# A two-layer hybrid decoder step on one core: the border chain in steps, the end of mixing reordered, the sampled convolution traced first

## The chip, the cores and the metric

The kernel runs on one core of a Trainium2 chip. The metric is the time of one execution in microseconds on the device; lower is better. The engines are PE (TensorE, matmuls), DVE (VectorE), ACT (ScalarE), POOL (GpSimd) and SP (SyncE, which here only issues DMAs).

## The reference

One inference step of a trunk of two layers. 512 prompt rows and 32 sampled rows (8 sequences of 4 tokens) go through the same weights. Each layer mixes tokens in four groups of width 256 (a convolution of width 31, a gated MLP, differential attention, pooling), projects the four back and adds; then follows a SwiGLU network of hidden width 2816.

```python
def hybrid_layer(x, pos, conv_prev, pool_prev, attend, lam_init, p):
    h = rms_norm(x, p['g_mix_pre'])
    z = h @ p['w_in']                                        # 1024 -> 2048
    a, ga, u, vb, q, k, v, xd = jnp.split(z, IN_SPLITS, axis=-1)
    ya, conv_new = conformer_conv(a, ga, conv_prev, ...)     # width 31, LayerNorm, silu
    yb, v_rows = chunk_sgu(gelu(u), gelu(vb), ...)
    o = attend(q, k, v, lam)
    yc = rms_norm(o, p['attn_sub_g'], LN_EPS) * (1.0 - lam_init)
    yd, pool_new = pool_mix(xd, pool_prev, pos, p['pool_w'], p['pool_scale'])
    mix = jnp.concatenate([ya, yb, yc, yd], axis=-1) @ p['w_out']
    x = x + rms_norm(mix, p['g_mix_post'])
    gate, up = jnp.split(rms_norm(x, p['g_ffn_pre']) @ p['w_gu'], 2, axis=-1)
    x = x + rms_norm((silu(gate) * up) @ p['w_down'], p['g_ffn_post'])
    return x, k, v, conv_new, pool_new, v_rows
```

The sampled rows use paged keys and values, and the last 30 convolution inputs and 15 pooling inputs of their sequences (`state_conv`, `state_pool`); the new states are outputs.

## The kernel before

Every product of float32 numbers is made of three: activations and weights are each split into a rounded part and the rest (`xhi`, `xlo`; `whi` by ACT, L194, and `wlo` by DVE or POOL, L197). `xhi` and `xlo` hold the activations of all 544 rows with the model dimension on the partitions: columns 0 to 511 are the prompt's four tiles of 128 rows, 512 to 543 the sampled rows. `turn` (L236 to 242) fills them for one tile: PE transposes, an ACT cast to `xhi`, a DVE subtraction to `xlo`.

The code is traced with Python generators that hand each other the turn. A planner in the compiler then draws up the order of each engine's queue: it takes what its own model says is ready, and among that what was traced first (`high_priority` moves work up). Every engine then works through its queue in order, and instructions wait on semaphores. So the place of a piece in the trace is a preference, not a position.

A layer has two stages. In `mixing` the prompt's 512 rows go through `w_in`, in halves: for each block of 128 output columns first the rows 0 to 255, then rows 256 to 543, with the sampled ones (`B0, BN = 256, 288`). Beside it run `conv`, `attention`, `gating` and `pooling`, one step at a time (`advance`); `conv` becomes urgent once its 60 taps (L427) are traced. Their outputs are `Y[0]` to `Y[3]` (ya, yb, yc, yd), split by `hilo` (ACT L351, DVE L352). At its end `conv` normalises four tiles (`xn`, L455), turns them back (L461), scales them and applies tanh (ACT L463, L464), and forms ya by a DVE product (L465). `pooling` adds windows for the two halves of its channels (L645), subtracts the mean (L662 to 665) and multiplies by a small matrix on PE. `gating` ends with a Gelu on ACT (L619) and the product u times gate (DVE L623).

The second stage is `prompt` with `sample` beside it. `project_last` makes `w_out` (eight turns of 24 matmuls; `W_OUT_TURNS` goes through tiles and halves, and within one, `W_OUT_ORDER`: yc, ya, yd, yb), with square (ACT L1299) and product by the gain (DVE L1300). After a tile's second half `finish` does the first norm (`ss`, `rsqrt`, x_t at L1318), squares (ACT L1323), does the second norm (L1326) and turns the tile. `rsqrt` is a DVE step (L177) and a power on POOL (L178). The weights of the second half go into a ring (`ring2`) in a pool that opens after mixing's. The gate and up blocks and `w_down` follow. After each piece the main loop moves `sample` on: `sample_conv`, `sample_gate` and `sample_pool` in rounds, then attention over the cache with gathers by POOL, then the sampled feed-forward part.

`sample_conv` loads two state pieces of 120 rows (tag `pr`, two buffers, shared with the other two), turns them (L875), forms the new inputs (L880), stores the new state rows (L886 to 890: a POOL copy, a PE turn, an ACT copy, a DMA), then does 60 taps on DVE (L894, L897) and a LayerNorm.

At the layer border the last `w_down` product ends with `finish` for each tile, and for the sampled rows with `finish_sample` (L244 to 265): a product with a selector adds four partial sums, then square and gain (L253, L254), first norm (L257), square (L261), second norm (L263) and the turn. It is traced after tile 3's `finish`; its inputs are there before. Then mixing of the next layer starts with four first halves; PSUM has two banks `acc` and two banks `s` for them.

## Time and profile before

| what | us |
|---|---|
| three timed runs | 1435.68, 1439.87, 1442.28 |
| their median | 1439.87 |
| the profiled execution | 1446.75 |
| its span, first to last instruction | 1445.1 |
| PE busy in it | 1389.1 |
| DVE busy | 818.4 |

The profile is one execution; its rows carry a start in microseconds from the span's start. Layer 0's mixing ends near 180 and its out-projection near 240; the border to layer 1 lies near 740; layer 1's mixing ends near 900.

### The profile page before, as it was taken

Reading aid. Unit: us, or ns where it says so; the run is one execution under the profiler, and the core shown is the slowest. Engines: PE = TensorE matmul, PEld = TensorE weight load, DVE = VectorE, ACT = ScalarE, POOL = GpSimd, SP = SyncE. Lnnn points to the kernel's source line nnn. Section 1 sums busy time; section 2 is a strip of 40 time slices with the busy share of each in tenths; the row PEclk is TensorE's granted clock in tenths of the full one; section 3 lists DMA queues with packets and bytes.
Section 4 is the critical chain, followed back from the end, with each engine's and each line's share of the span. In section 5 each row is a group of like instructions: output and inputs, shape, how many; then the busy total and the mean of one; then the engine's idle time right before and its main releaser. Section 6 shows DMA issues by size and latency. Waiting matters only on the chain.

```text
span 1445.1 us, 22960 instructions
## 1 busy us (share of the span) xinstructions
PE 1389.1 (96%) x9274; PEld 1089.5 (75%) x9274; DVE 818.4 (57%) x1652; ACT 488.9 (34%) x962; POOL 213.5 (15%) x245
## 2 busy tenths in 40 slices
PE   6999798999999999999979997999999999999997
PEld 6987687876666777777879876888766667778775
DVE  5996677876433233333759856778664332333345
ACT  4346543332233222222433454334222332222231
POOL 1001124454200000000000011244442000000000
PEclk9999899999999999999989978999999999999999
DMA  7320334889768721314522203367876796213132
GB/s 215 96 89 30 127 130 158 295 319 330 246 215 272 225 91 59 117 59 150 188 69 75 74 30 125 128 218 264 330 293 241 222 296 213 71 61 114 59 135 91
DMA packets 155171, 235.60 MB, mean 163 GB/s; under 512 B 8880, under 2 KB 116346, under 8 KB 155066
## 3 DMA queue, kind: packets, MB, share of 16 engines
q1 hardware_dynamic: 130378, 157.34, 33.5%
q0 software_dynamic: 18496, 67.18, 12.7%
q10 hardware_dynamic: 6192, 9.61, 1.8%
q8 instruction: 73, 1.20, 0.3%
q14 instruction: 32, 0.26, 0.1%
HBM read 222.07 MB, written 12.04 MB: 162 GB/s over the span
## 4 chain that ended last, share of the span: by engine, by line
PE 81%; DVE 8%; DMA 4%; issue 3%; ACT 2%; POOL 2%; SPq 0%; POOLq 0%; DVEq 0%; ACTq 0%
PE acc L128 63%; PE sx L128 9%; PE ps L128 3%; PE s L128 3%; DMA kr<-in_cache_k_dram,ik 2%; DVE sca L897 2%; PE oT L128 1%; DMA vr<-in_cache_v_dram,iv 1%; DVE wlo L197 1%; PE ps L521 1%; POOL kr L1011 1%; DVE xlo L242 1%; PE ps L239 1%; DVE m L1326 1%; DVE x_t L1318 1%
## 5 line engine op out<-in xcount | busy, mean ns | idle before, releaser
L128 PE MATMUL acc<-xhi,whi 128*128 128x512 f32 (+2 forms) x1152 | 408.8, 356 | 1.1 <-ACT zs L403 0.8
L128 PE MATMUL acc<-xlo,whi 128*128 128x512 f32 (+2 forms) x1152 | 405.0, 352 | 1.1 <-DVE xlo L242 1.1
L128 PE MATMUL acc<-xhi,wlo 128*128 128x512 f32 (+2 forms) x1152 | 405.8, 353 | 0.0
L194 ACT CAST whi<-raw 128x1024 fp32r<-128x1024 f32 x178 | 184.7, 1048 | 378.3 <-PE acc L128 349.1
L197 DVE TENSOR_TENSOR wlo<-raw,whi 128x1024 fp32r<-128x1024 f32 x172 | 214.8, 1255 | 170.8 <-ACT whi L194 169.1
L128 PEld LDWEIGHTS acc<-xhi,whi 128*128 128x128 f32 x1152 | 219.2, 191 | 44.4 <-issue 11.2
L128 PEld LDWEIGHTS acc<-xhi,wlo 128*128 128x128 f32 x1152 | 219.2, 190 | 33.0 <-issue 6.8
L128 PEld LDWEIGHTS acc<-xlo,whi 128*128 128x128 f32 x1152 | 219.5, 191 | 31.5 <-issue 3.9
L128 PE MATMUL acc<-whi,h 128*128 128x512 f32 x704 | 223.7, 396 | 0.0
L128 PEld LDWEIGHTS acc<-whi,h 128*128 128x128 f32 x704 | 131.1, 188 | 42.9 <-issue 9.5
L178 POOL TENSOR_TENSOR rsw<-rsw,mhalf 128x1 f32<-128x1 f32 (+2 forms) x62 | 36.6, 594 | 795.1 <-DVE rsw L177 769.3
L128 PE MATMUL acc<-wlo,h 128*128 128x512 f32 x352 | 138.2, 394 | 0.0
L1014 DVE STREAM_TRANSPOSE kt<-kr 128x1024 f32<-128x1024 f32 x64 | 78.0, 1232 | 23.6 <-DMA kr<-in_cache_k_dram,ik 19.5
L427 DVE SCALAR_TENSOR_TENSOR cacc<-hext,pf,cacc 128x512 f32<-128x512 f32 x120 | 86.7, 746 | 0.7
L1011 POOL DMA_INDIRECT kr<-in_cache_k_dram,ik x64 | 69.4, 1084 | 88.0 <-DVE kt L1014 71.5
L128 PEld LDWEIGHTS acc<-wlo,h 128*128 128x128 f32 x352 | 66.1, 188 | 17.7 <-issue 4.1
L1370 DVE SCALAR_TENSOR_TENSOR th<-th,acc 128x512 f32<-128x512 f32 (+1 forms) x46 | 29.7, 646 | 85.2 <-PE acc L128 85.1
L1041 POOL DMA_INDIRECT vr<-in_cache_v_dram,iv x64 | 62.5, 977 | 71.5 <-PE sx L128 55.1
L128 PE MATMUL sx<-vr,pt 128*32 128x256 f32 x512 | 46.5, 383 | 1.2 <-DMA vr<-in_cache_v_dram,iv 1.2
L1179 DVE SCALAR_TENSOR_TENSOR sth<-sth,ps 128x64 f32<-128x64 f32 x22 | 4.8, 220 | 71.4 <-ACT sth L1178 71.4
L128 PE MATMUL sx<-kt,qs 128*32 128x128 f32 x1024 | 43.9, 277 | 0.7 <-DVE kt L1014 0.7
L1372 ACT CAST h<-th 128x512 fp32r<-128x512 f32 (+1 forms) x48 | 27.9, 582 | 48.3 <-DVE th L1370 48.2
(426 smaller groups left out, 1790.3 us busy)
## 6 DMA issues: line engine op xcount, KB each, us to landing
raw<-in_w_gu_dram SPq DMA_DIRECT2D x44, 1024.0 KB
raw<-in_w_down_dram SPq DMA_DIRECT2D x20, 1024.0 KB
rws<-in_w_gu_dram SPq DMA_DIRECT2D x40, 512.0 KB
raw<-in_w_in_dram SPq DMA_DIRECT2D x16, 1024.0 KB
raw<-in_w_out_dram SPq DMA_DIRECT2D x8, 1024.0 KB
rwo<-in_w_out_dram SPq DMA_DIRECT2D x16, 512.0 KB
rws<-in_w_down_dram SPq DMA_DIRECT2D x16, 512.0 KB
x<-x_t ACTq DMA_DIRECT2D x12, 512.0 KB
```

What stands on the lines that cost most here:

```text
L128: T.matmul(out, lhsT, rhs, start=start, stop=stop)
L178: G.tensor_tensor(y, v, mhalf[:P, :n], op=ALU.pow)
L194: S.copy(hi, src)
L197: eng.tensor_tensor(lo, src, hi.bitcast(F32), op=ALU.subtract)
L239: T.transpose(ov[:, c, :], src[:P, 128 * (4 * b + c):128 * (4 * b + c) + 128], ident[:P, :P])
L427: V.scalar_tensor_tensor(a, hext[c][:, t:t + SEQ], pf[:, 8 + 2 * t + c:9 + 2 * t + c], a, op0=ALU.mult, op1=ALU.add)
L897: V.scalar_tensor_tensor(a[:, c], ext[:, c, :, t:t + 4], pf[:, 8 + 2 * t + c:9 + 2 * t + c], a[:, c], op0=ALU.mult, op1=ALU.add)
L1011: G.indirect_dma_start(out=kr, out_offset=None, in_=ck, in_offset=bass.IndirectOffsetOnAxis(ap=ik[:, s, bg:bg + 1], axis=0))
L1014: V.transpose(kt, kr)
L1041: G.indirect_dma_start(out=v.rearrange("p t e -> p (t e)"), out_offset=None, in_=cv, in_offset=bass.IndirectOffsetOnAxis(ap=iv[:, s, a:a + ...
L1370: V.scalar_tensor_tensor(th[:, :n], th[:, :n], 0.5, ou[:, :n], op0=ALU.mult, op1=ALU.mult)
L1372: S.copy(hh, th[:, :n])
```

## The change

Four things. `finish_sample` becomes a generator of six steps, and at the border of layer 0 these are traced between the steps of tile 3's `finish` (`beside`). In `pooling` the first two adds of the second half of the channels are queued behind conv's last normalised tile on DVE, and traced after it. In `gating` the last products and their splits are traced after conv's last ya product and queued behind it on DVE. `issue_after` sets an order within one queue only, without a wait for the end. In `sample_conv` both states are loaded in one round, the taps come ahead of the stores of the state rows, and there are three rounds of taps and not seven. The extra buffers of `rsw` for the tag `q` keep the two chains' roots apart.

```diff
--- before.py
+++ after.py
@@ -172,7 +172,7 @@
 
     def rsqrt(pool, src, P, n, scale, eps, tag):
 
-        w = pool.tile([128, 2, n], F32, tag=f"rs{tag}{n}", bufs={"m": 4, "p": 3}.get(tag, 1) if n == 1 else 1, name="rsw")
+        w = pool.tile([128, 2, n], F32, tag=f"rs{tag}{n}", bufs={"m": 4, "p": 3, "q": 2}.get(tag, 1) if n == 1 else 1, name="rsw")
         v, y = w[:P, 0, :], w[:P, 1, :]
         V.tensor_scalar(v, src, scale, eps, op0=ALU.mult, op1=ALU.add)
         G.tensor_tensor(y, v, mhalf[:P, :n], op=ALU.pow)
@@ -244,6 +244,10 @@
     def finish_sample(fp, parts, m_s, x_t, stage, gpo, gpr, dst, tag):
 
 
+        for _ in finish_sample_steps(fp, parts, m_s, x_t, stage, gpo, gpr, dst, tag):
+            pass
+
+    def finish_sample_steps(fp, parts, m_s, x_t, stage, gpo, gpr, dst, tag):
         ss = fp.tile([128, 4], F32, name="sums_s")[:NT]
         junk = fp.tile([128, DM], BF16, name="junk_s")
         for half in range(2):
@@ -252,15 +256,20 @@
             hs = slice(512 * half, 512 * half + 512)
             S.activation(junk[:NT, hs], o[:NT, :], AF.Square, accum_out=ss[:, half:half + 1])
             V.tensor_tensor(m_s[:, hs], o[:NT, :], gpo[:NT, hs], op=ALU.mult)
+        yield
         V.tensor_tensor(ss[:, 2:3], ss[:, 0:1], ss[:, 1:2], op=ALU.add)
         r = rsqrt(fp, ss[:, 2:3], NT, 1, 1.0 / DM, RMS_EPS, tag)
+        yield
         V.scalar_tensor_tensor(x_t, m_s, r, x_t, op0=ALU.mult, op1=ALU.add)
         SY.dma_start(x_at(stage + 1)(SEQ, NT), x_t)
         if gpr is None:
             return
         S.activation(junk[:NT], x_t, AF.Square, accum_out=ss[:, 3:4])
+        yield
         r = rsqrt(fp, ss[:, 3:4], NT, 1, 1.0 / DM, RMS_EPS, tag)
+        yield
         V.scalar_tensor_tensor(m_s, x_t, r, gpr[:NT], op0=ALU.mult, op1=ALU.mult)
+        yield
         if dst is None:
             turn(m_s, NT, SEQ)
             return
@@ -452,7 +461,9 @@
                 for c in range(2):
                     T.transpose(o[:, 128 * c:128 * c + 128], out[c][:, 128 * t:128 * t + 128], ident)
                 mean, r = ln_stats(mp, o[:, :256], 128, "m")
-                V.tensor_scalar(xn[:, t, :], o[:, :256], mean, r, op0=ALU.subtract, op1=ALU.mult)
+                flow["xn"] = V.tensor_scalar(xn[:, t, :], o[:, :256], mean, r, op0=ALU.subtract, op1=ALU.mult).ins
+                if t == 3:
+                    done.add("xn")
                 yield
             y = yp.tile([128, 2, 2, SEQ], F32R, tag="y", name="ya")
             for c in range(2):
@@ -462,8 +473,10 @@
                 zh, th = out[c], hext[c][:, 0:SEQ]
                 S.activation(zh, o, AF.Identity, scale=pf[:, 72 + c:73 + c], bias=pf[:, 74 + c:75 + c])
                 S.activation(th, zh, AF.Tanh)
-                V.scalar_tensor_tensor(zh, th, 1.0, zh, op0=ALU.add, op1=ALU.mult)
+                flow["za"] = V.scalar_tensor_tensor(zh, th, 1.0, zh, op0=ALU.add, op1=ALU.mult).ins
                 hilo(y, c, zh)
+                if c == 1:
+                    done.add("za")
                 yield
             Y[0] = y
 
@@ -618,10 +631,13 @@
                 yield
             S.activation(uv[:, 0:2], uv[:, 0:2], AF.Gelu)
             S.activation(zs[:, 4:6, :], zs[:, 4:6, :], AF.Gelu)
+            while "za" not in done:
+                yield
             for c in range(2):
                 tf = uv[:, 2 + c, :]
-                V.tensor_tensor(tf, tf, uv[:, c, :], op=ALU.mult)
-                hilo(y, c, tf)
+                with tc.issue_after(flow["za"]):
+                    V.tensor_tensor(tf, tf, uv[:, c, :], op=ALU.mult)
+                    hilo(y, c, tf)
                 yield
             Y[1] = y
 
@@ -647,6 +663,11 @@
                 d = dext[c]
                 s2 = mp.tile([128, 528], F32, tag="pl", bufs=3, name="s2")
                 wn = mp.tile([128, 528], F32, tag="pl", bufs=3, name="wn")
+                held = ExitStack()
+                if c == 1:
+                    while "xn" not in done:
+                        yield
+                    held.enter_context(tc.issue_after(flow["xn"]))
                 if c == 0:
                     add(s2[hi, 0:526], d[hi, 0:526], d[hi, 1:527])
                     add(wn[lo, 0:SEQ], d[lo, 14:526], d[lo, 15:527])
@@ -655,6 +676,7 @@
                     add(s2[:, 0:526], d[:, 0:526], d[:, 1:527])
                     s4 = mp.tile([128, 528], F32, tag="pl", bufs=3, name="s4")
                     add(s4[:, 0:524], s2[:, 0:524], s2[:, 2:526])
+                    held.close()
                     add(wn[lo, 0:SEQ], s4[lo, 8:520], s4[lo, 12:524])
                     add(s2[hi, 0:520], s4[hi, 0:520], s4[hi, 4:524])
                     add(wn[hi, 0:SEQ], s2[hi, 0:SEQ], s2[hi, 8:520])
@@ -875,10 +897,18 @@
                 T.transpose(o[:, 120 * c:120 * c + 120], st[:, 128 * c:128 * c + 128], ident[:120, :120])
             for c in range(2):
                 S.copy(ext[:, c, 4 * hf:4 * hf + 4, 0:30], o[:, 120 * c:120 * c + 120].rearrange("p (s t) -> p s t", s=4))
-            yield
         for c in range(2):
             V.scalar_tensor_tensor(ext[:, c, :, 30:34], zs[:, 2 + c, :].rearrange("p (s t) -> p s t", s=NS), 1.0,
                                    zs[:, c, :].rearrange("p (s t) -> p s t", s=NS), op0=ALU.add, op1=ALU.mult)
+        a = mp.tile([128, 2, NS, 4], F32, tag="sca", name="sca")
+        for c in range(2):
+            V.tensor_scalar(a[:, c], ext[:, c, :, 0:4], pf[:, 8 + c:9 + c], pf[:, c:c + 1], op0=ALU.mult, op1=ALU.add)
+        for t in range(1, CW):
+            for c in range(2):
+                V.scalar_tensor_tensor(a[:, c], ext[:, c, :, t:t + 4], pf[:, 8 + 2 * t + c:9 + 2 * t + c], a[:, c],
+                                       op0=ALU.mult, op1=ALU.add)
+            if t % 10 == 0:
+                yield
         for hf in range(2):
             o = ps()
             for c in range(2):
@@ -889,15 +919,6 @@
             S.copy(cn[:120, :256], o[:120, :256])
             S.dma_start(O[8][l, 4 * hf:4 * hf + 4].rearrange("s t c -> (s t) c"), cn[:120, :256])
             yield
-        a = mp.tile([128, 2, NS, 4], F32, tag="sca", name="sca")
-        for c in range(2):
-            V.tensor_scalar(a[:, c], ext[:, c, :, 0:4], pf[:, 8 + c:9 + c], pf[:, c:c + 1], op0=ALU.mult, op1=ALU.add)
-        for t in range(1, CW):
-            for c in range(2):
-                V.scalar_tensor_tensor(a[:, c], ext[:, c, :, t:t + 4], pf[:, 8 + 2 * t + c:9 + 2 * t + c], a[:, c],
-                                       op0=ALU.mult, op1=ALU.add)
-            if t % 4 == 0:
-                yield
         o = ps()
         for c in range(2):
             T.transpose(o[:NT, 128 * c:128 * c + 128], a[:, c].rearrange("p s t -> p (s t)"), ident)
@@ -1302,13 +1323,15 @@
             if half == 1:
                 yield from tail(t)
 
-    def finish(fp, jp, m, sums, t, stage, g, tag="ps"):
+    def finish(fp, jp, m, sums, t, stage, g, tag="ps", beside=None):
 
         x_t = fp.tile([128, DM], F32, tag="xio", bufs=2, name="x_t")
         SY.dma_start(x_t, x_at(stage)(128 * t, 128))
         ss = sums[t]
+        step = (lambda: None) if beside is None else (lambda: next(beside, 0))
         V.tensor_tensor(ss[:, 2:3], ss[:, 0:1], ss[:, 1:2], op=ALU.add)
         r = rsqrt(fp, ss[:, 2:3], 128, 1, 1.0 / DM, RMS_EPS, "p")
+        step()
         if g is None and t == 3:
             for i, eng in enumerate((SY, S)):
                 hs = slice(512 * i, 512 * i + 512)
@@ -1321,10 +1344,14 @@
             return
         junk = jp.tile([128, DM], BF16, tag="ft", bufs=2, name="junk")
         S.activation(junk, x_t, AF.Square, accum_out=ss[:, 3:4])
+        step()
         S.dma_start(x_at(stage + 1)(128 * t, 128), x_t)
         r = rsqrt(fp, ss[:, 3:4], 128, 1, 1.0 / DM, RMS_EPS, "p")
+        step()
         V.scalar_tensor_tensor(m[t], x_t, r, g, op0=ALU.mult, op1=ALU.mult)
+        step()
         turn(m[t], 128, 128 * t, tag)
+        step()
         yield 0.0
 
     def prompt(l, fp, share):
@@ -1394,15 +1421,18 @@
                         if half == 1 and k0 + nk == NF:
                             y = yp.tile([128, 2, DM], F32, tag="y", name="ysm")
                             SY.dma_start(y[:NT, 1, :], x_at(2 * l + 1)(SEQ, NT))
-                            share["end"] = lambda: finish_sample(tp, m4, y[:NT, 0, :], y[:NT, 1, :], 2 * l + 1, gpo, gpr, None, "p")
+                            share["end"] = finish_sample_steps(tp, m4, y[:NT, 0, :], y[:NT, 1, :], 2 * l + 1, gpo, gpr, None,
+                                                               "p" if gpr is None else "q")
                             if gpr is None:
-                                share.pop("end")()
+                                for _ in share["end"]:
+                                    pass
                     return run
 
                 def tail(t):
-                    yield from finish(tp, fp, m, sums, t, 2 * l + 1, gpr)
-                    if t == 3 and "end" in share:
-                        share["end"]()
+                    beside = share["end"] if t == 3 and gpr is not None else None
+                    if beside is not None:
+                        next(beside)
+                    yield from finish(tp, fp, m, sums, t, 2 * l + 1, gpr, "ps", beside)
 
                 yield from project_last(tp, fp, A["w_down"][l], f0, nf, act, m, False, gpo, sums,
                                         ((ring2, None), (ring2, ring2)), tail, None, also)
```

## Rows read from the trace of the kernel before

**Rows 1.** The page's first section: busy time, share of span, instructions.

```profile
PE 1389.1 (96%) x9274; PEld 1089.5 (75%) x9274; DVE 818.4 (57%) x1652; ACT 488.9 (34%) x962; POOL 213.5 (15%) x245
```

**Rows 2.** The page of PE's waits: released by; us in total, times, longest.

```profile
PE ps L239 <- DVE ysm L263: 7.1, 1, 7.1
...
PE sx L239 <- DVE m L1326: 6.4, 4, 2.8
```

**Rows 3.** Engines by stretch: length, busy us (instructions) per engine, granted clock, DMA share, GB/s.

```profile
177.00:181.80 4.80, 4.78 (x11) 3.81 (x12) 2.70 (x6) 3.80 (x6) 1.15 (x1) 0.50 0.54 198
...
181.80:187.70 5.90, 5.90 (x27) 4.81 (x26) 5.19 (x3) 2.31 (x4) 4.61 (x2) 1.00 0.01 4
...
240.00:243.30 3.30, 3.30 (x18) 3.20 (x16) 1.34 (x3) 0.56 (x2) 0.00 (x0) 0.50 0.00 0
...
742.60:748.50 5.90, 5.90 (x25) 5.90 (x25) 0.73 (x3) 0.27 (x1) 0.00 (x0) 0.50 0.12 30
...
948.50:960.00 11.50, 8.36 (x67) 7.67 (x66) 11.16 (x32) 4.40 (x14) 2.24 (x4) 1.00 0.58 185
...
837.20:854.30 17.10, 17.10 (x66) 14.36 (x67) 8.80 (x26) 8.24 (x20) 1.83 (x2) 0.50 0.19 63
...
121.60:138.70 17.10, 17.10 (x109) 12.96 (x110) 12.35 (x37) 12.24 (x31) 2.39 (x3) 1.00 0.18 63
```

**Rows 4.** Timeline, mixing's end: start, us, instruction, idle time before and its releaser.

```profile
170.86 1.37 PE L128 MATMUL acc<-wn,pw 128*128 128x512 f32 x2 [2.47 <-DVE wn L665]
...
172.27 0.69 ACT L668 ACTIVATE wn<-acc,pf 128x512 f32<-128x512 f32 x1 [2.81 <-PE acc L128]
...
177.02 0.80 PE L128 MATMUL acc<-whi,ya 128*128 128x512 f32 x1 [3.22 <-ACT ya L351]
...
179.53 3.89 ACT L194 CAST whi<-raw 128x1024 fp32r<-128x1024 f32 x4 [1.00 <-DVE ya L352]
```

**Rows 5.** Timeline of PE at the layer border.

```profile
725.77 1.04 PE L239 MATMUL ps<-cst,m 128*128 128x128 f32 x8
...
732.61 1.90 PE L128 MATMUL ps<-m4h,cst 128*32 128x512 f32 x4 [0.96 <-DVE xlo L242]
...
741.61 1.06 PE L239 MATMUL ps<-cst,ysm 32*128 32x32 f32 x8 [7.10 <-DVE ysm L263]
```

**Rows 6.** Engines by stretch, the out-projection of layer 0.

```profile
187.40:208.20 20.80, 20.80 (x106) 16.89 (x105) 14.20 (x55) 6.53 (x18) 3.23 (x6) 1.00 0.51 174
...
208.20:241.40 33.20, 27.43 (x167) 23.54 (x166) 32.75 (x99) 15.22 (x35) 10.20 (x13) 0.98 0.43 137
```

**Rows 7.** Timeline of DVE at the border: tile 3's last splits, the sampled norm.

```profile
731.86 1.29 DVE L242 TENSOR_TENSOR xlo<-ps,xhi 128x512 fp32r<-128x512 f32 x2 [1.43 <-ACT xhi L241]
...
740.29 1.27 DVE L263 SCALAR_TENSOR_TENSOR ysm<-ysm,rsw,g_g_mix_pre 32x1024 f32<-32x1024 f32 x1 [0.71 <-POOL rsw L178]
```

**Rows 8.** Timeline of DVE at mixing's end.

```profile
165.29 1.38 DVE L645 TENSOR_TENSOR wn<-s 64x512 f32<-64x512 f32 x2
...
169.46 1.26 DVE L623 TENSOR_TENSOR uv<-uv 128x512 f32<-128x512 f32 x2
...
171.66 1.06 DVE L455 TENSOR_SCALAR xn<-ps,ag,rsw 128x256 f32<-128x256 f32 x2 [0.58 <-POOL rsw L178]
```

**Rows 9.** Engines by stretch, tile 3's chain at the border.

```profile
723.20:733.20 10.00, 8.82 (x71) 7.95 (x70) 6.16 (x11) 3.18 (x6) 1.10 (x2) 1.00 0.13 53
```

**Rows 10.** The taps alone (L897) by stretch: length, DVE busy (instructions), clock, DMA.

```profile
208.20:241.40 33.20, 15.76 (x60) 0.98 0.43 137
```

**Rows 11.** Timeline of DVE and POOL in the out-projection.

```profile
217.35 4.74 POOL L197 TENSOR_TENSOR wlo<-raw,whi 128x1024 fp32r<-128x1024 f32 x2
...
217.44 4.69 DVE L897 SCALAR_TENSOR_TENSOR sca<-scx,pf,sca 128x32 f32<-128x32 f32 x2
...
222.06 1.27 DVE L1318 SCALAR_TENSOR_TENSOR x_t<-m,rsw,x_t 128x1024 f32<-128x1024 f32 x1
...
237.38 1.28 DVE L1326 SCALAR_TENSOR_TENSOR m<-x_t,rsw,g_g_ffn_pre 128x1024 f32<-128x1024 f32 x1
```

## The prediction

> **What bounds it now.** The page's first section comes first: the tensor engine (PE) is busy 1389.1 of 1445.1 us [rows 1]. A change that takes no matmul away can only win time in which PE stands still or runs slow. PE's waits, by what ended them, come next [rows 2]: one of 7.1 us at the layer border ends with the sampled rows' norm (L263), and four in the out-projection, 6.4 us together, end with the prompt's second norm (L1326). The third view is the granted clock by stretch [rows 3]: behind such waits PE goes on at the lower of its two levels, 1.2 GHz. Half of a slow stretch is lost: 2.95 us of 5.9 at the border, 2.4 of 4.8 at the end of mixing, 1.65 of 3.3 in the out-projection. The fourth is the order of work around the end of mixing, where PE waits 2.47 us for pooling and 3.22 us for the first piece of ya [rows 4], and layer 1 repeats it. So what can be won here is: border 8.1 of waits (0.96 and 7.10 [rows 5]) + 2.95; mixing's end 2 x (5.7 + 2.4); out-projection 5.8 [rows 6] + 1.65 in layer 0, and in layer 1 3.1 of waits (8.36 us busy of 11.50 [rows 3]) and a slow stretch alike, 4.8: about 39.5 us.
>
> **Border.** PE's next matmuls want columns 256 to 543, so both tile 3 and the sampled rows must be normed and turned. Today these follow one another: the last split of tile 3 ends at 733.15 [rows 7], only at 732.61 does PE start the product that opens the sampled chain, and that chain ends with a turn at 741.61 [rows 5]. From 732.61 to the restart at 742.60 [rows 3] are 10.0 us, all serial. The change lays these links between those of tile 3. It adds no instruction; the price is that they share queues. The vector engine gets two products by the gain (0.69 each, half of the pair in [rows 8]), two norms of 1.27 [rows 7] and three small sums (0.15 each): 4.4 us. Between 723.2 and 733.2 it is busy 6.16 of 10.0 us [rows 9], so 3.84 are free, in pieces. Tile 3 is delayed by 0.5 us (4.4 - 3.84) at best and 4.4 (nothing fits) at worst; I take 1.5, near the lower end, because the free pieces lie where the vector engine waits for a square or a root, and there a link of the other chain can go. Behind each waiting link now stands a link of the other chain on the vector queue, and on the scalar queue the casts of the turn stand behind the sampled square (L261); only these two chains wait for that, so it is within the 1.5. Tile 3 is then ready at 734.65, the sampled turn a split later, near 735.2: 7.4 us earlier. Of the 2.95 us of slow clock I give 1.8 back, since much shorter waits also left 3.3 us at half clock in the out-projection [rows 3]. Taken: 8.5. Lower bound: the opening product stays behind the turn of tile 2 (725.77 [rows 5]) and gets its banks when that is evacuated, some 3 us on; then the 10.0 us chain ends near 739: 3.6. Upper bound: 8.4 + 2.95 = 11.3. In the last layer the chain runs as before: nothing.
>
> **Mixing's end.** Ahead of the last xn (ends at 172.72) the vector queue holds pooling's two window sums (1.38), its mean and edges (about 1.07) and the gating products (1.26) [rows 8]. All that goes behind, 3.7 us, so xn ends near 169.0. From there to ya's first matmul (177.02) the rest of the chain took 4.3 us [rows 4]: ya comes at 173.3. What is late next is yd. Behind xn now stand pooling's five adds (0.69 each: 3.5), mean and edges (1.07) and two ya products (like the gating's, 1.26): 5.9 us, then PE's pooling product (1.37) and two scalar passes (0.69 each) [rows 4]: 177.7. PE has 12 ya matmuls to do meanwhile. 24 matmuls of yd and yb are left of the first two turns, 5.2 us at 0.2185 each (27 in 5.9 [rows 3]): done at 182.9 against 187.7 today, 4.8 won; with a half clock as today perhaps 2.5. The weights of the second half are next: their first cast, at 179.53, waits for the last ya split [rows 4]. If its buffer frees with ya, they come before PE asks for them. If it frees with the last split of all (10.4 us of vector work behind xn: pooling 4.6, yd 0.69, four pairs of 1.28; so 179.5 to 180.5), nothing is won. With pooling's adds last on the vector queue yd comes at 183, and the end is 188.3: 0.6 lost. Between -0.6 and 4.8 I take 2.75 a layer, 5.5 in all. Three of the adds fill idle vector time today and lose that cover; this is in the sum.
>
> **Out-projection.** All 60 taps of layer 0 lie between 208.2 and 241.4, 15.76 us of vector time [rows 10], in a stretch where the vector engine is busy 32.75 of 33.2 us; from 187.4 to 208.2 it stands idle 6.6 us [rows 6]. Traced first, the taps can start once the states are turned, near 190. 11.3 us of the 15.76 are work; 4.4 is one tap standing still [rows 11]. 6.6 us fit into idle time, the rest pushes index arithmetic back. The later stretch then holds 26.6 us of work in 33.2. Tile 3's second norm starts at 237.38 today [rows 11], 12.3 us behind the last product (225.1); its own links (two norms of 1.28, a gain product, squares and roots) need some 7 before it, and 2 to 3 us of weight splits come between: 235 instead of 237.4, and tile 2 more. PE arrives earlier too, so 2 us of waits stay. Of 12.2 us in both layers I take 6. The moved loads: the second state takes the buffer that the gate's rows (L834) took, so these wait on SP's queue until the first state is turned, and the prompt's rows and the next weights stand behind them; SP issues those later than that today. The moved stores (pool copy, turn, scalar copy and DMA) go later, and nobody waits for them. Bounds: -1 (a tap ahead of an evacuation, though three banks give PE 10 us) to 12.2.
>
> One row speaks against this. The tap that stood still did so from 217.44 to 222.1 while the pool engine split weights from 217.35 to 222.09, and x_t of tile 2 came right behind it [rows 11]. If any vector instruction waits there, taking the tap away frees nothing for tile 2, and 3.5 us are won in place of 6. The Trainium skill has this as a rule (SBUF — State Buffer, "Who interferes with whom"): a vector instruction with two SBUF inputs and a pool instruction that reads SBUF exclude each other for a whole instruction. By it x_t, with two such inputs, inherits the stall, and the total would be 2.5 us less. The pair of rows agrees with it.
>
> **Sum.** 8.5 + 5.5 + 6 = 20.0 us. Against the profiled execution (span 1445.1, 1446.75 with what surrounds it) that is 1426.7; it lies 6.9 us over the median of the runs, 1439.87. One thing may explain that: from 837.2 to 854.3 PE ran at half clock, 66 matmuls where the same stretch of layer 0 has 109 [rows 3], 6.7 us. Whether other runs have it is not shown. From the median the forecast is 1419.9, called 1420.
>
> **Rivals.** First, only the border pays: yd comes as late as ya did, and the vector engine stays the bound of the out-projection through the pool stall. For it: 5.9 us of work behind xn, and [rows 11]; against: the idle 6.6 us. Gain 8.5 to 9: 1431. Second, the change doesn't do what it says: a planner draws up the order on each engine, trace order is only its preference, and it may fill the sampled links late again or put the taps where they stand now. Only the two holds are fixed. Then some 1436, by the border's lower end. Third, slower, by one mechanism in mixing's tail: pooling goes last, and the second half's weights take the buffer that its last split frees. That split ends near 184, so the first cast comes 4.5 us behind 179.53, PE stands from 188.3 to 192.1, and as behind the border's 7.10 us wait a stretch at half clock follows, up to 5.1 us: 9.6 a layer, 19.2. It outweighs the 14.5 us of the other two once a layer loses over 7.25, that is with the cast behind 182.2 and the slow clock, or behind 186.8 without. Net 1444.6. For it: the cast waits for mixing's last split today; against: ya is that split, and the holds bring it forward.
>
> **How the numbers follow.** Forecast 0.60 (its own range 1410 to 1428), border alone 0.22 (1428 to 1434), nothing 0.12 (1432 to 1441), slower 0.06. All lower bounds together give 1438.5, all upper ones 1406.8. With a scatter of 3.5 us either way (1435.68 to 1442.28 before) the range is 1408 to 1436. Half a per cent, 7.2 us, is about what can be told from no change: faster means under 1432.7. The forecast, three quarters of the second case and a little of the third: 0.78; 0.17 within; 0.05 slower.
>
> **What would show it.** Border: the 7.10 us wait gone, the opening product ahead of tile 3's turn, PE back some 3 us behind that turn. Mixing: the last xn 3.7 us sooner, and PE's longest wait there ends with yd. Out-projection: taps in the stretch that answers to 190 to 208, waits for L1326 under 2 us. It would be wrong with the first weight cast later than today, counted from mixing's last w_in matmul, or with a new half-clock stretch of 17 us, which moves the time by 6.7 either way whatever the change does.

## The result, and the profile after

The changed kernel takes 1463.0 us (median of four runs, 1460.97 to 1467.93), the kernel before, in the same set, 1437.8 (four runs): a ratio of 1.015, interval 1.011 to 1.019 (the two medians alone give 1.018, 25.3 us). Forecast were 1420 us, 1408 to 1436. The profiled execution after took 1467.93 us, its span 1466.2 against 1445.1.

The page's first section, after, and then the view of PE's waits (released by; us in total, times, longest):

```profile
PE 1403.8 (96%) x9274; PEld 1088.9 (74%) x9274; DVE 816.1 (56%) x1652; ACT 489.2 (33%) x962; POOL 217.4 (15%) x245
```

```profile
PE sx L128 <- DMA vr<-in_cache_v_dram,iv: 9.2, 6, 3.0
PE acc L128 <- ACT ya L360: 7.4, 2, 3.7
PE ps L239 <- DVE ysm L271: 4.9, 1, 4.9
...
PE acc L128 <- ACT yd L360: 2.9, 2, 1.4
PE acc L128 <- DVE ya L361: 2.5, 2, 1.3
PE ps L917 <- DVE sca L908: 2.5, 1, 2.5
...
PE sx L239 <- DVE m L1351: 0.5, 2, 0.3
```

PE does the same 9274 matmuls in 14.7 us more [rows 1]. The prompt's second norm (now L1351) is down from 6.4 us to 0.5, the sampled norm from 7.1 to 4.9 [rows 2]; in their place stand value gathers of the sampled attention, yd, a second wait for ya, and a stored state (L917).

To see where the time went, I cut each profiled execution at equal counts of columns of the prompt's weight matmuls (products with whi or wlo; 2,245,632 columns in every kernel). A stage lasts from the start of the matmul at one cut to that at the next; the last one ends at 2240 thousand. The other columns are experiments, told below: x1 is the border alone, x2 the two holds at mixing's end alone, x3 the new order of the sampled convolution alone, x4 the same with as many steps of trace as before, y2 the hold in gating alone, z2 the two holds with one pass moved to another engine, z3 the old order of the convolution with fewer steps, z4 the border with its opening product early, and the hold in gating. One column is one execution, and executions of the same kernel differ: the whole change, profiled three times, has 63.3, 63.2 and 61.1 at mixing's end. Layer 1's mixing also holds a half-clock stretch of 0 to 17 us that comes and goes between executions (before has it: [rows 3], 837.2).

| stage (thousand columns) | before | after | x1 | x2 | x3 | x4 | y2 | z2 | z3 | z4 |
|---|---|---|---|---|---|---|---|---|---|---|
| start, 0–180 | 116.1 | 117.6 | 116.3 | 117.5 | 117.8 | 117.6 | 117.7 | 117.7 | 117.6 | 117.2 |
| mixing's end 0, 180–240 | 59.1 | 63.3 | 59.0 | 63.3 | 59.3 | 59.3 | 58.7 | 60.9 | 59.0 | 60.2 |
| out-projection 0, 240–340 | 60.8 | 59.6 | 59.2 | 59.1 | 61.3 | 61.6 | 58.7 | 59.1 | 54.2 | 58.8 |
| attention, FFN 0, 340–1120 | 465.9 | 475.2 | 483.2 | 476.9 | 480.1 | 478.6 | 479.2 | 463.2 | 472.9 | 470.0 |
| border, 1120–1180 | 45.3 | 43.0 | 43.1 | 45.1 | 44.4 | 44.9 | 44.7 | 45.0 | 45.2 | 37.5 |
| mixing 1, 1180–1360 | 150.1 | 151.4 | 143.5 | 148.2 | 142.5 | 146.6 | 140.3 | 148.4 | 143.5 | 142.9 |
| out-projection 1, 1360–1460 | 57.9 | 55.6 | 58.3 | 59.3 | 58.7 | 59.0 | 56.9 | 59.0 | 53.0 | 60.1 |
| attention, FFN 1, 1460–2240 | 465.7 | 476.3 | 474.3 | 478.4 | 481.0 | 475.8 | 478.0 | 467.6 | 479.0 | 464.4 |

Of the 21.1 us between the two profiles, 19.9 lie in the two attention stages (9.3 + 10.6), 4.2 in layer 0's mixing end; the border gave 2.3, the out-projections 1.2 and 2.3.

Equal prompt columns are not equal work, though. In after, 18 matmuls that prepare the sampled attention have moved from each attention stage into the out-projection ahead of it (out-projection 0 ends at 249.3 in before, at 254.0 in after). Timeline of PE, before and then after:

```profile
254.90 1.87 PE L128 MATMUL ps<-zs,se 128*128 128x32 f32 x16
```

```profile
249.83 1.87 PE L128 MATMUL ps<-zs,se 128*128 128x32 f32 x16
```

With two more behind them PE spends 1.85 us on these (249.83 to 251.68). At equal work the out-projections of after won 3.0 and 4.1 us, 7.2 together, and the attention stages lost 11.1 and 12.5, 23.6 together. Every run with the new order and 6 steps (x3 in the table) has these 18 moved; z3 and all others have not.

The two attention stages, before and then after (stretch, length, then per engine busy us and instructions: PE, weight loads, vector, scalar, pool; granted clock, DMA share, GB/s):

```profile
249.30:715.20 465.90, 465.11 (x3093) 345.39 (x3092) 221.92 (x388) 134.51 (x225) 70.75 (x71) 1.00 0.58 198
968.60:1434.30 465.70, 464.32 (x3093) 344.78 (x3092) 219.22 (x386) 130.05 (x219) 64.65 (x68) 1.00 0.56 189
```

```profile
254.00:729.10 475.10, 468.66 (x3074) 343.56 (x3073) 217.59 (x371) 133.74 (x221) 64.63 (x66) 1.00 0.56 188
979.20:1455.50 476.30, 471.10 (x3075) 343.54 (x3075) 216.99 (x384) 129.59 (x217) 66.04 (x67) 0.99 0.54 183
```

PE stands still 2.2 us in the two of before and 11.6 in those of after: 9.5 of the 23.6. Half of 10.2 us at the lower clock (below) is 5 more. The other 9 are not explained: PE is busy for longer with fewer matmuls.

The second loss is at mixing's end. First two rows of before that [rows 4] doesn't have, the last `w_in` matmul and the first of the second half's; then the timeline of after (start, us, instruction, idle time before and its releaser):

```profile
165.33 0.29 PE L128 MATMUL acc<-xhi,wlo 128*128 128x288 f32 x1
...
187.58 0.40 PE L128 MATMUL acc<-whi,yc 128*128 128x512 f32 x1
```

```profile
177.44 0.80 PE L128 MATMUL acc<-whi,ya 128*128 128x512 f32 x1 [3.72 <-ACT ya L360]
...
186.62 1.02 PE L128 MATMUL acc<-wn,pw 128*128 128x512 f32 x2
...
187.67 0.69 ACT L690 ACTIVATE wn<-acc,pf 128x512 f32<-128x512 f32 x1 [7.64 <-PE acc L128]
...
188.92 3.89 ACT L194 CAST whi<-raw 128x1024 fp32r<-128x1024 f32 x4
...
193.27 0.40 PE L128 MATMUL acc<-whi,yc 128*128 128x512 f32 x1
```

These answer to [rows 4]: pooling's product and scalar pass, then 170.86 and 172.27, now come behind ya, and the second half's first cast follows them at 188.92 in place of 179.53. The second half's matmuls start at 193.27 (before: 187.58). After runs 3.05 us later here already (its last `w_in` matmul starts at 168.38), so counted from that matmul the cast is 6.3 us later and the second half 2.6.

The border on PE, answering to [rows 5], and the engines by stretch (length, busy us per engine, granted clock, DMA share, GB/s): 176.0, 754.4, and the two places where value gathers are waited for:

```profile
739.72 1.04 PE L239 MATMUL ps<-cst,m 128*128 128x128 f32 x8
...
744.13 1.05 PE L128 MATMUL ps<-m4h,cst 128*32 128x512 f32 x2
...
753.53 1.03 PE L239 MATMUL ps<-cst,ysm 32*128 32x32 f32 x8 [4.92 <-DVE ysm L271]
```

```profile
176.00:186.20 10.20, 7.50 (x17) 5.43 (x18) 6.51 (x13) 2.57 (x5) 0.00 (x0) 0.50 0.60 207
...
754.40:759.70 5.30, 5.30 (x24) 5.24 (x24) 0.76 (x3) 0.29 (x2) 0.00 (x0) 0.50 0.14 37
290.80:298.90 8.10, 2.56 (x29) 1.02 (x32) 3.13 (x12) 0.81 (x2) 4.60 (x5) 1.00 0.98 360
298.90:302.30 3.40, 3.38 (x30) 1.48 (x34) 0.00 (x0) 0.00 (x0) 0.00 (x0) 0.50 1.01 397
1020.20:1029.30 9.10, 5.85 (x44) 2.65 (x44) 2.79 (x8) 1.19 (x3) 1.95 (x4) 0.63 0.88 340
```

The opening product still stands behind tile 2's turn. In the attention, PE works 2.56 of 8.1 us while the DMA engines are full (share 0.98), and goes on at half clock; in layer 1 the stretch of 9.1 us has a mean clock of 0.63, that is 6.8 us of it at half.

### The profile page after: what moved, and what is told of

Read it like the earlier page. It is cut to its first block, busy times and chain, and to the rows that moved or that the text cites. A ratio compares the mean times of both kernels' runs of the same rounds, so it can differ in the third digit from the quotient of the medians.

```text
span 1466.2 us, 22969 instructions
## 1 busy us (share of the span) xinstructions
PE 1403.8 (96%) x9274; PEld 1088.9 (74%) x9274; DVE 816.1 (56%) x1652; ACT 489.2 (33%) x962; POOL 217.4 (15%) x245
## 5 line engine op out<-in xcount | busy, mean ns | idle before, releaser
L178 POOL TENSOR_TENSOR rsw<-rsw,mhalf 128x1 f32<-128x1 f32 (+2 forms) x62 | 39.6, 640 | 780.2 <-DVE rsw L177 764.0
L128 PE MATMUL sx<-vr,pt 128*32 128x256 f32 x512 | 54.2, 406 | 9.3 <-DMA vr<-in_cache_v_dram,iv 9.2
L128 PE MATMUL sx<-kt,qs 128*32 128x128 f32 x1024 | 47.9, 280 | 2.2 <-DVE kt L1035 2.1
L128 PEld LDWEIGHTS sx<-vr,pt 128*32 128x32 f32 x512 | 20.8, 115 | 30.3 <-issue 15.8
L128 PEld LDWEIGHTS sx<-kt,qs 128*32 128x32 f32 x1024 | 31.0, 110 | 16.2 <-issue 9.4
```

Of the source, the lines that this page charges most:

```text
L128: T.matmul(out, lhsT, rhs, start=start, stop=stop)
L178: G.tensor_tensor(y, v, mhalf[:P, :n], op=ALU.pow)
```

## Experiments

All ratios are to the kernel before, run in the same set. It took 1438 us in the first set and 1442 in that of the z runs, but 1463 to 1466 in the four others (x, y, w, v), so ratios are compared, not times.

### The parts alone

x1: the border in steps only (finish_sample_steps, beside, tag q).

> Before plus the border in steps alone (finish_sample_steps, beside, the tag q). Prediction on record: 8.5 us faster, lower end 3.6. New theory, from the trace of after: the opening product still stands behind the turn of tile 2 and waits for its banks, so from the last product of w_down to the restart of PE it goes from 26.1 us to about 24, that is 2 to 3 us faster and nothing elsewhere. Rival: the late layers lose from the steps too (queues shared), then no gain or a loss of 1 to 2 us.

Measured 0.9969 (0.994 to 1.000), 4.5 us; the border stage 43.1. The order on PE there is that of after (opening product at 746.15, tile 2's turn at 741.74; the 4.93 us wait for the sampled norm). The new theory holds for the border stage, 2.2 us: the lower end of the forecast, or less.

x2: the two holds only, at pooling and at gating:

```diff
+                if c == 1:
+                    while "xn" not in done:
+                        yield
+                    held.enter_context(tc.issue_after(flow["xn"]))
...
+                with tc.issue_after(flow["za"]):
```

> Before plus the two holds at mixing's end alone (pooling's sums and mean behind the last xn, gating's products behind ya). Prediction on record: 5.5 us faster. New theory, its third rival: ya starts 2.6 us sooner but yd and the first cast of the second half's weights come some 9 us later, 5 us lost in layer 0 and 4 in layer 1, so 8 to 10 us slower. Rival: the loss at mixing's end in after comes from the sampled convolution being traced first, then this one is 0 to 5 us faster.

Measured 1.0075 (1.005 to 1.010), 11 us; mixing's end 63.3, as in after. w4, the same kernel in another set:

> The two holds at mixing's end alone. 8 to 11 us slower in any set (1.0055 to 1.0075), since no gather takes part in it. Against the variant with pooling's pass on the vector engine (1.0032): the difference, 3 to 6 us, is what the scalar queue costs.

Measured 1.0046 (1.001 to 1.008). The loss is confirmed, its size 7 to 11 us. Against z2 (1.0032, below) the difference is 2 us and inside the intervals, not the 3 to 6 that were expected.

x3: the new order of the sampled convolution only; x4: the same with the steps of trace padded back from 6 to 12 (the edit of x4 against x3):

```diff
+            yield
...
-            if t % 10 == 0:
+            if t % 4 == 0:
```

> Before plus the sampled convolution in its new order alone (taps first, state stores behind, 6 steps of trace in place of 12). Prediction on record: 6 us faster. New theory: the out-projection wins 2 to 3 us a layer, but with fewer steps the whole sampled attention is traced earlier against the prompt's matmuls, PE takes its products before their gathers have landed, and each layer loses about 9 us: 12 to 14 us slower in all. Rival: the attention's loss in after comes from mixing's end being late, then this one is 4 to 6 us faster.

> As the one with the new order of the sampled convolution alone, but with 12 steps of trace as before (a step behind each state, a step every four taps). If the number of steps is what moves the attention: no loss there, 3 to 6 us faster than before. If it is the order of the taps or the stores themselves that delays the gathers: as slow as the unpadded one, 12 to 14 us slower.

Measured 1.0041 (1.002 to 1.007) and 1.0021 (1.000 to 1.004): 6 and 3 us slower (the 3 just within the noise), neither the 13 nor the gain. The product of the parts, 0.9969 x 1.0075 x 1.0041, is 1.0085. y1 and w1, the whole in two more sets:

> The changed kernel itself once more, beside the parts. If the parts add: 0.9969, 1.0075 and 1.0041 (border, mixing, convolution) make 1.0085, some 12 us slower on the chip of those runs. If what was lost in the attention hangs on how fast the gathers land on a chip: 1.015 as in the first runs where the kernel before takes 1438 us, near 1.008 where it takes 1465 us and has those waits in its own attention already.

> The changed kernel once more, in one set with its parts. Where before takes 1440 us: 1.013 to 1.017. Where it takes 1465 us: 1.006 to 1.010.

Measured 1.0078 (1.004 to 1.011) and 1.0097 (1.006 to 1.013): y1 is what the parts of x make, w1 lies above what x1 and the parts of its own set make (0.9969 x 1.0046 x 1.0036 = 1.0051), with intervals that meet. In the first set the whole was 1.015. Why less is lost here is argued, since before has no profile in a longer set: x1, in the order of before until the border, already needs 483.2 us for the first attention stage, against 465.9. Its list of PE's waits has entries that before and z1 don't have:

```profile
PE sx L128 <- issue: 9.5, 20, 1.1
...
PE acc L128 <- issue: 1.8, 6, 0.4
```

PE waits for nothing that is shown, 12.1 us in all with a smaller entry; y1 has 11.3 us alike. If before pays this too, less is left for the change to lose: against x1 the attention stages of y1 are 480.7 in layer 0 and 478.6 in layer 1, 2.5 less and 4.3 more.

### Mixing's end: which hold, and what the cast waits for

y2: the gating hold alone. y3: the pooling hold alone.

> Before plus the hold of the gating products behind ya alone. New theory (pooling behind the last xn is what delays yd and, behind it, the first cast of the second half's weights): this hold alone is harmless, ya starts about 1 us sooner and the kernel is 0 to 3 us faster. Rival: the gating's splits, now behind ya, delay that cast as much: 8 to 10 us slower.

> Before plus the hold of pooling's last sums and mean behind the last xn alone. New theory: this carries the whole loss of the two holds, some 8 to 10 us slower (yd's first product about 9 us later than before against ya, the first cast of the second half behind it). Rival (the loss needs both holds): within 3 us of before.

Measured 0.9973 (0.994 to 1.001) and 1.0023 (0.999 to 1.006). The gating hold does no harm. The pooling hold alone loses less than both together (its layer 0 stage 60.9), with runs from 1460 to 1476, and its interval holds no change: that it carries the whole loss isn't shown. Counted as below, from the last `w_in` matmul, its third turn starts 0.8 us later than that of before, and with both holds 2.0 to 2.6: that speaks for the rival, the loss needs both.

In x2 the vector engine ends ya's last split at 181.78 (first row, two of 0.64); on the scalar queue the cast stands behind pooling's pass. z2 takes that pass and the high half of its split to the vector engine:

```diff
...
+                else:
+                    V.tensor_scalar(wn[:, 0:SEQ], o, pf[:, 6 + c:7 + c], None, op0=ALU.mult)
+                    V.tensor_copy(y[:, 0, c, :], wn[:, 0:SEQ])
+                    V.tensor_tensor(y[:, 1, c, :], wn[:, 0:SEQ], y[:, 0, c, :].bitcast(F32), op=ALU.subtract)
```

> The two holds at mixing's end, with pooling's scalar pass and the high half of its split (second pair only) on the vector engine in place of the scalar engine. Theory: the first cast of the second half's weights was free at ya's last split (181.8 us in the run with both holds alone) and stood 7.6 us behind pooling's scalar pass in the scalar queue; then the cast comes near 182, the third turn some 4 to 6 us sooner after ya, and the kernel is within 3 us of before. Rival: the buffer, not the queue, held it: the cast stays near 189 and the kernel 8 to 10 us slower.

Timelines (vector and scalar engine) of x2, then (scalar, PE, vector) of z2:

```profile
180.50 1.28 DVE L352 TENSOR_TENSOR ya<-cacc,ya 128x512 fp32r<-128x512 f32 x2
...
188.15 0.69 ACT L681 ACTIVATE wn<-acc,pf 128x512 f32<-128x512 f32 x1 [7.64 <-PE acc L128]
...
189.39 3.89 ACT L194 CAST whi<-raw 128x1024 fp32r<-128x1024 f32 x4
```

```profile
180.13 3.89 ACT L194 CAST whi<-raw 128x1024 fp32r<-128x1024 f32 x4 [1.32 <-DVE ya L352]
...
184.84 1.02 PE L128 MATMUL acc<-wn,pw 128*128 128x512 f32 x2
...
185.90 0.75 DVE L685 TENSOR_SCALAR wn<-acc,pf 128x512 f32<-128x512 f32 x1 [4.51 <-PE acc L128]
```

The cast now comes 0.04 us behind the end of ya's last split (178.81 + 1.28 on the vector engine) in place of 7.6: the queue held it, not the buffer. The Trainium skill (TensorE: Matmul & The Clock Gate, "Architectural detail") says that the scalar and vector queues are strictly first in, first out; this pair agrees. The kernel is at 1.0032 (1.001 to 1.005), 4.6 us slower than before.

Did PE wait for the cast? In layer 0, no. The last `w_in` matmul, the cast and the first matmul of the third turn, in w4 (the holds alone) and then in z2, whose cast is the row above:

```profile
168.34 0.29 PE L128 MATMUL acc<-xhi,wlo 128*128 128x288 f32 x1
...
188.24 3.89 ACT L194 CAST whi<-raw 128x1024 fp32r<-128x1024 f32 x4
...
192.59 0.40 PE L128 MATMUL acc<-whi,yc 128*128 128x512 f32 x1
```

```profile
167.17 0.29 PE L128 MATMUL acc<-xhi,wlo 128*128 128x288 f32 x1
...
191.37 0.40 PE L128 MATMUL acc<-whi,yc 128*128 128x512 f32 x1
```

The third turn starts 24.25 us behind the last `w_in` matmul in w4 (24.90 in x2, the same kernel) and 24.20 in z2, though the cast comes at 19.9 in the one and at 13.0 in the other; in before it starts at 22.25. The 2.0 us between are nearly all waits of PE that have changed. Before has 5.7 us of them there (2.5 for pooling, 3.2 for ya [rows 4]). With the holds they are 7.6: 1.2 for xn, 3.7 for ya, 1.3 for ya's second part and 1.4 for yd. In z2 the last two remain (1.25 and 1.30), since pooling's product reaches PE at 184.84, behind 18 matmuls of ya and yd. Only in layer 1 does x2 have a wait for whi, one of 1.0 us, and z2 has none.

That the stage falls from 63.3 to 60.9 is for the most part not the cast's doing: x2 has a stretch at half clock ahead of the last `w_in` matmul, which z2 and before have not, and y2 without the pooling hold has.

```profile
149.20:152.60 3.40, 3.40 (x17) 3.40 (x16) 0.55 (x1) 0.46 (x1) 0.22 (x1) 0.50 0.00 0
```

Layer 1's mixing can be compared between x1 and x2, which have the same granted clock there:

```profile
774.30:917.80 143.50, 134.98 (x965) 116.04 (x965) 112.75 (x248) 70.95 (x165) 15.08 (x15) 0.95 0.23 76
```

```profile
775.90:924.10 148.20, 135.91 (x966) 116.05 (x965) 109.53 (x247) 70.92 (x164) 12.30 (x15) 0.95 0.23 74
```

The holds lose 4.7 us there.

### The convolution: order or steps

z3 keeps the old order and takes steps away (none behind the states, one every ten taps: 6 in place of 12):

```diff
-            yield
...
-            if t % 4 == 0:
+            if t % 10 == 0:
```

> The sampled convolution in its old order, but with 6 steps of trace in place of 12. If the number of steps alone makes the loss of the new order (1.0041): 4 to 8 us slower, value gathers waited for by PE. If the order (taps first, stores behind) makes it: within 2 us of before.

Measured 1.0045 (1.002 to 1.007). Its stages are the sharpest of all: the out-projections win 6.6 and 4.9 us, the attention stages lose 7.0 and 13.3. The engines by stretch of z3, for [rows 6]; then the span of its taps (count; ns least/median/most; first and last start); then its wait for gathers:

```profile
187.40:208.20 20.80, 20.80 (x96) 16.86 (x95) 20.04 (x81) 7.03 (x18) 4.72 (x9) 1.00 0.49 164
208.20:241.40 33.20, 32.38 (x215) 28.20 (x214) 29.51 (x74) 15.98 (x37) 13.67 (x16) 1.00 0.48 159
```

```profile
L896 DVE SCALAR_TENSOR_TENSOR sca<-scx,pf,sca x60: 207/242/2132, 193.8 to 219.1; 128x32 f32<-128x32 f32 x60
```

```profile
PE sx L128 <- DMA vr<-in_cache_v_dram,iv: 7.3, 7, 2.5
```

With half the steps the taps run from 193.8, the vector engine is busy 20.04 of 20.8 us where it was 14.20, and PE 32.38 of 33.2 where it was 27.43. The taps traced first, but in 12 steps (x4), stay where they were, 211.1 to 239.7. So the steps move the taps, and they also move the attention: PE waits 7.3 us for value gathers in place of 1.2. Early taps alone don't make z3's gain: in x3 they run from 194.0 as well, and its out-projections, without the 18 moved matmuls, take 59.5 and 56.8 us (x1: 59.2 and 58.3).

Is the new order harmless, then, once padded? w2, w3 and v1, v2 repeat x3 and x4 in two sets:

> The new order of the sampled convolution alone. Where before takes 1440 us and its attention has no waits: PE waits for value gathers, both layers together 10 to 16 us slower (1.007 to 1.011), so that with the holds it makes up the whole. Where before takes 1465 us: 1.004 again.

> The new order of the sampled convolution with 12 steps as before. If the few steps are the cause: within 2 us of before where before takes 1440 us, under half of the unpadded one's loss in any case. If the order is: as the unpadded one.

> The new order of the sampled convolution, 6 steps. In a set where before takes 1440 us: 1.006 to 1.011 if it carries what the whole lost in the attention; 1.003 to 1.005 if steps are all there is to it. In a set with 1465 us: 1.004 once more.

> The same order with 12 steps. In a set where before takes 1440 us: within 0.2 per cent of before if the steps are the cause, as the unpadded one if the order is. In a set with 1465 us: 1.004, no better than the unpadded one.

Measured 1.0036 (1.000 to 1.007) and 1.0057 (1.003 to 1.009), then 1.0042 (1.001 to 1.008) and 1.0017 (0.999 to 1.004). Padding wins in two sets and loses in one; the pair is not told apart. The form with 6 steps is slower than before in all three sets, the padded one clear of noise only in w3. The padded form's own cost shows in its out-projection (three profiles 61.6 to 62.1, ten in the old order and 12 steps 57.8 to 60.8), in PE's waits within that stage (x4) and then, by line, on the vector engine (busy, mean ns):

```profile
PE sx L239 <- DVE m L1326: 2.8, 1, 2.8
PE ps L896 <- POOL scf L895: 1.4, 1, 1.4
PE ps L896 <- DVE th L1370: 1.0, 1, 1.0
```

```profile
L887 DVE SCALAR_TENSOR_TENSOR sca<-scx,pf,sca 128x32 f32<-128x32 f32 x60 | 13.7, 279 | 0.0
L1318 DVE SCALAR_TENSOR_TENSOR x_t<-m,rsw,x_t 128x1024 f32<-128x1024 f32 x4 | 7.3, 1820 | 1.3 <-POOL rsw L178 1.3
```

The stored states' turns (L896), now late, stand in PE's queue and wait for pool copies and banks, 2.4 us with the prompt's matmuls behind them. And the taps won 2.2 us against x1 (13.7 for 15.9) while x_t lost as much (7.3 for 5.1).

### The border with its opening product early

y4 takes the opening products to another bank and ahead of tile 2's norm (the edit against x1):

```diff
-            o = ps()
+            o = psx("sx" if tag == "q" else "ps")
...
-                    if beside is not None:
-                        next(beside)
+                    if t == 2 and gpr is not None:
+                        next(share["end"])
```

z1 is x1 and y2 together, z4 is y4 and y2 together.

> Border in steps, but the opening products of the sampled sums are traced ahead of tile 2's norm and take banks that no turn holds. In the plain form they stand behind tile 2's turn and PE comes back 24 us behind the last w_down product. If that place is what kept the gain at 4.5 us: the prediction's 8.5 us are won, and the restart comes some 20 us behind. Rival: the vector queue, on which both chains stand, is the limit: 4 to 5 us as in the plain form, PE waiting on the sampled norm still.

> Border in steps and the gating hold, without the pooling hold and without the new order of the convolution. If the parts add: 0.9969 x 0.9973 = 0.994, some 8 us faster than before. Rival: each of the two gained only by the chance of where the attention's gathers fell, and together they give 0 to 3 us.

> Border in steps with the opening products ahead of tile 2's norm and on other banks, and the gating hold. The profile of the early form without the hold showed PE waiting under 2 us at the border, some 8 us less than before, and the 6 us over the plain form lost again in mixing and attention of layer 1. If that loss belongs to the early form: as the plain border with the hold or slower. If it was that one arrangement of layer 1: 3 to 4 us faster than the plain border with the hold, 0.990 to 0.992.

PE at the border in z4, and the half clock behind it:

```profile
710.53 1.90 PE L128 MATMUL sx<-m4h,cst 128*32 128x512 f32 x4
...
737.69 1.04 PE L239 MATMUL ps<-cst,m 128*128 128x128 f32 x8
739.69 0.43 PE L239 MATMUL ps<-cst,ysm 32*128 32x32 f32 x4 [0.96 <-DVE xlo L242]
```

```profile
741.20:744.60 3.40, 3.40 (x16) 3.40 (x16) 0.22 (x2) 0.00 (x0) 0.00 (x0) 0.51 0.00 0
```

The border stage falls to 37.5 us in y4 and z4, 7.8 under before: the wait is 0.96 us, 2 us behind tile 3's turn, and 3.4 us of half clock stay. But 1.8 of the 7.8 is work that moved: the four opening matmuls now stand ahead of the stage's first cut (710.53 to 712.37 in z4). At equal work the border wins 6.0. PE is back 18.9 us behind the last w_down product (before 26.1, x1 24.1), as expected of y4.

Yet y4 as a whole is at 1.0000 (0.997 to 1.003), z1 at 0.9982 (0.996 to 1.000), z4 at 0.9972 (0.996 to 0.999). So z1 gained 2.6 us, as its rival said, and not the 8 of the sum; and z4 fell between its two cases. z4 is the fastest kernel here, 4 us under before, and only 0.7 under z1. From z1's profile to z4's the border wins 5.9 and attention 0 loses 2.7, of which 1.8 is that moved work; the start of layer 1's mixing (1180 to 1260) loses 1.5, and mixing's end of layer 0 1.1. In y4 layer 1's mixing and out-projection lose 7.7 against x1 (148.9 and 60.6); y4 is 6.8 us longer at half clock there, which costs some 3.4. The gain at the border is real; that later stages give it back is seen, what in their new order does it isn't settled.

## Why the prediction was wrong

The time went the other way, past the slowest of the three rivals (1444.6). Two steps failed. One put nothing for the number of trace steps that the change takes away, and the attention stages lost 23.6 us. The other took pooling to run through at once behind xn, and mixing's end lost where it was to win.

**Border, 8.5 forecast.** (Its own terms, 7.4 + 1.8, make 9.2.) The mechanism was right, the place of one product wrong. The opening product stayed behind tile 2's turn, the case named as the lower bound (3.6); 2.3 us came. With that product early, 6.0 come at equal work. The half clock that was to shrink by 1.8 us stayed 5.3 of 5.9 behind the 4.92 us wait and fell to 3.4 only behind 0.96.

**Mixing's end, 2.75 a layer forecast; 4.2 lost in layer 0.** xn's last piece did end sooner, at 173.23, but only 2.5 us sooner as counted from the end of the last w_in matmul (4.6 us behind it, before 7.1), not 3.7. The step that failed is the one behind it: "Behind xn now stand ... 5.9 us, then PE's pooling product". It took pooling to run through at once. On the vector engine pooling's adds alternate with the two ya products, then the gating products and ya's split come, and the mean is whole at 182; on PE the product then stands behind 18 matmuls, nearly all at half clock (0.50 in the stretch at 176.0), and comes at 186.62. yd was forecast for 177.7 and came at 189.06. So PE's waits behind the last w_in matmul grew from 5.7 to 7.6 us. Most of the rest of the 4.2 is slow clock: after, like x2, has 3.4 us of it near 149, which kernels without the holds have too (y2).

The two bounds for the cast were both on ya's and the last split's buffer; it stood in the scalar queue behind pooling's pass. The sign that the prediction named for being wrong came, the cast later than before counted from the last w_in matmul. The third rival, with a chance of 0.06, had the right event (pooling last, the cast late: 4.5 us forecast, 6.3 measured so, 9.4 by the clock) by the wrong cause, a buffer, and with the wrong price: PE did not stand for it in layer 0.

**Out-projection, 6 forecast; 7.2 came at equal work** (3.0 + 4.1). The size is luck: the forecast put it down to the taps being traced first, and what moves them is the number of steps: in x4 they lie late. In z3, with few steps in the old order, 6.6 and 4.9 are won, near the upper bound of 12.2 for both layers. "The moved stores go later, and nobody waits for them" is false: PE does, 2.45 us for L917 in after. The row that spoke against holds in x4 and z3: x_t took the stall over (in x4 one of 3.43 us, the others 1.27 to 1.29, while the pool engine split weights from 220.69 for 5.82 us). The Trainium skill's rule (SBUF — State Buffer, "Who interferes with whom") agrees with that. In after a tap stood still (2.28 us), not x_t. In before it was two taps, 4.69 us together ([rows 11] has x2), and not one.

**What was missing.** The diff takes 12 steps of the sampled convolution to 6, and the sampled attention is traced behind these steps. The prediction costed what the steps contain, and not that fewer of them bring forward everything traced behind, against the prompt's matmuls. The gathers hardly came sooner by it: in after, the first starts at 244.72 (before 245.81), while PE is some 5 us behind, and the value products come upon gathers under way. This term was put at nothing, and 23.6 us came: z3, with this alone, loses 20.3 there (and wins 11.5 in front). That the steps account for all of it in after is argued, since the new order wasn't measured in a set where before takes 1440 us; and of the 23.6, 9 are neither waits nor slow clock.

**The sum.** Forecast -20.0, came +21.1 between the profiles: the border 6.2 short, mixing's end 9.7 (5.5 forecast for both layers, 4.2 lost in layer 0), the out-projection 1.2 better, 23.6 that stood in no term, and 2.8 at the start (1.5) and in layer 1's mixing (1.3). The start's 1.5 is scatter: the same kernel has 116.0 in w1. Layer 1's 1.3 hides the holds' 4.7 (x2 against x1), since the profile of before was longer at half clock there (mean clock 0.91, after 0.93).

## What to carry to other kernels

When a background flow is traced in steps against a main one, its number of steps is part of the schedule: changing it moves everything that is traced behind, gathers included, so list what comes after the flow before costing what is in it. A step that is put last on one engine is late on every queue that it passes; follow it to each in-order queue (here vector, PE, scalar) and ask what unrelated work stands behind it there. Then ask whether anyone waits for what is late: the cast came 6 us later, and PE waited nothing for it in one layer and 1.0 us in the other. And a gain at one place is worth only what the next stages don't give back: take the stages apart at equal work before believing a local row, and count the instructions of each, since a piece that crosses a cut looks like a gain on one side and a loss on the other.

## What the runs showed of the hardware

All 14 profiles of the four longer sets have 8.2 to 14.7 us of PE's waits put down to issue, none over 1.1 us; the six of the two shorter sets have none. What makes them isn't shown, nor what the rest of the 24 us is. The chip alone doesn't: the sets x, v (longer) and z (shorter) ran on the same one.

The slow clock (1.2 GHz, granted 0.50) behind a wait doesn't shrink in step with it: at the border 5.9 us of it follow the 7.10 us wait of before [rows 3], 5.3 the 4.92 of after, 3.4 the 0.96 of z4.
